# A two-layer attention and mixture-of-experts block on one core: another PSUM bank for one pair of transposes, another issuing engine for eight stores

## Chip, cores and metric

The kernel runs as one program on one core of a Trainium2 chip. The metric is the device time of one execution in microseconds (us); several executions are timed and their median is taken. The names of the engines are those of the profile: PE is TensorE (PEld its weight loads), DVE is VectorE, ACT is ScalarE, POOL is GpSimd, SP is SyncE, which does nothing here but issue DMAs.

## What is computed

512 tokens of width 1024 pass through two layers. Each layer is a token mixer followed by a hierarchical mixture of experts; both are added to the tokens through gates that come from a conditioning vector. The first layer mixes with sliding-window attention and gated linear attention, the second with block attention. The change touches only the norm in front of the experts and the experts themselves:

```
for layer in range(2):
    shift1, scale1, gate1, shift2, scale2, gate2 = split(silu(c) @ ada_w[layer] + ada_b[layer], 6)
    h = rms(x, norm1_w[layer]) * (1 + scale1) + shift1
    x = x + gate1 * mixer[layer](h)
    h = rms(x, norm2_w[layer]) * (1 + scale2) + shift2
    # router: softmax over 4 groups, the best group; in it the best 2 of 8 experts, softmax over the two
    # each expert e of 32, on the tokens that chose it:
    #     y = (silu(h @ w1[e]) * (h @ w3[e])) @ w2[e]          # 1024 -> 512 -> 1024
    x = x + gate2 * sum over the two experts of (gate * y)
```

All values are 32-bit floats. The weights of one expert are 6 MB, those of all experts of one layer 192 MB.

## The kernel before

**Tiling.** The tokens stay in SBUF as `x_t`, four tiles of 128 tokens x 1024. Every expert has a window of 64 slots; two experts make a pair of 128 slots, and a pair's tokens are gathered from a DRAM copy of the normed tokens, `h2d[layer]`, by their numbers.

**The norm in front of the experts** is `norm2` (L574 to L590), called once for each of the four token tiles in each layer. It squares and sums (L576), takes the inverse root (L222 to L228), transposes the tile and copies the transposes out of PSUM (L582), multiplies by the router weights (L586, L587), then writes the normed tile into `t` (L589), a tile of a pool that holds it once under the name `adaacc`, and stores it to `h2d` (L590), 512 KB a time. Since there is one such tile, the L589 of a token tile waits until the store of the tile before it has landed. Before the change the store is issued from ACT's queue. This part, like the attention, is ordered by a scheduler.

**The experts** (L1344 to L1386) are ordered by hand: what is written is what each engine gets. The loop runs over `e` = 0 to 32 (number 32 is a second window of one full expert); `odd = e % 2`, and `pr = e // 2` is the pair. In one pass:

1. `stage1` (L1159): the tokens of the expert by w1 and w3 into the PSUM bank `h13`; then Silu on ACT (L1358).
2. `flip_rows` (L1128): four transposes (L1131) of one half of the *next* pair's tokens into the bank `tr`; four modulations on ACT (L1124) read them out, scaled and shifted, into `xT`.
3. Where `odd`: `gather` for the pair after next (L1107): four small matmuls (L1111) into the bank `num` give the slot numbers, DVE reads them (L1113), and GpSimd issues the indirect DMA (L1115) out of `h2d`.
4. DVE multiplies the Silu by the other half of `h13` (L1365): the gated values `gt`.
5. `combine` 0 and 1 of the expert before: PE (L1197) scatters its outputs into one of four banks `cmb`, and DVE adds them into the tokens (L1200).
6. `flip_hidden` (L1162): two transposes of `gt` (L1166) into a PSUM bank that the caller names, and a copy out of it on DVE (L1168), `gT`. Then `combine` 2 and 3.
7. `stage2` (L1174): `gT` by w2 (L1180) into the bank `py`, scaled on DVE (L1184). Between that and the split into two parts (ACT L1190, POOL or DVE L1191) stand `combine` 4 to 7 and, in every even pass, `flip_sel` (L1143): four transposes (L1147) into the bank `tr`, read by ACT (L1151) and DVE (L1152).

PSUM has eight banks here, all taken: `py`, `h13`, `num` and `tr` once each, `cmb` four times. A bank that is asked for again waits for the readers of what it held.

**The weights** come by 1 MB loads (L178, L181) on SP's queue into a ring of 18 slots, six for each expert, so the stream runs three experts ahead; a slot's next load is issued when its last matmul is done.

Of the kernel before, what the change touches and what calls it, by code (L numbers as in the profile page):

```python
# [74 lines left out]
def tile_hybrid_block(ctx, tc, a, out):  # L75
    nc = tc.nc
    V, S, G, PE, SP = nc.vector, nc.scalar, nc.gpsimd, nc.tensor, nc.sync
# [56 lines left out]
    h2d = [dram.tile([T, D], F32, name=f"h2d{l}") for l in range(2)]  # L134
# [83 lines left out]
    def rsqrt(sm, ss, n, inv, tag, out=None):  # L218
        v = sm.tile([P, n], F32, name=f"rv_{tag}")
        y = sm.tile([P, n], F32, name=f"ry_{tag}")  # L220
        t = sm.tile([P, n], F32, name=f"rt_{tag}")
        V.tensor_scalar(v, ss, inv, 1e-6, op0=OP.mult, op1=OP.add)  # L222
        S.activation(t, v, AF.Ln)
        S.activation(y, t, AF.Exp, scale=-0.5)
        V.scalar_tensor_tensor(t, y, -0.5, y, op0=OP.mult, op1=OP.mult)
        V.tensor_tensor(t, t, v, OP.mult)
        r = y if out is None else out
        V.scalar_tensor_tensor(r, t, 1.5, y, op0=OP.add, op1=OP.mult)  # L228
        return r
# [95 lines left out]
    def transpose_to(ps, blocks, name="pa"):  # L325
        t = ps.tile([P, 512], F32, name=name)
        for i, b in enumerate(blocks):
            PE.transpose(t[:, 128 * i:128 * i + 128], b, ident)
        return t


    for l in range(2):
        s1, s2 = "left", "right"
        tiles = ((0, 1, 2, 3), (3, 2, 1, 0))[l]
        with ExitStack() as att:
# [92 lines left out]
            with ExitStack() as ln:  # L428
# [54 lines left out]
                for k in range(KT):  # L483
# [4 lines left out]
                    t = tmp.tile([P, T], F32, name="ht", bufs=2)  # L488
# [85 lines left out]
            def norm2(tmp, i):  # L574
                ss = sm.tile([P, 1], F32, name="ss2")
                S.activation(tmp.tile([P, D], F32, name="xn2"), x_t[:, i, :], AF.Square, accum_out=ss)  # L576
                rsqrt(sm, ss, 1, 1.0 / D, "l2", out=r2[:, i:i + 1])
                xT = []
                for q in range(2):
                    t = com.tile([P, 4, 128], F32, name=("raw", ("stg", "pt")[l])[q], bufs=2 + l * q)  # L580
                    p = transpose_to(ppA, [x_t[:, i, 512 * q + 128 * k:512 * q + 128 * k + 128] for k in range(4)])
                    (V.tensor_copy, S.copy)[q](t, p.rearrange("p (k t) -> p k t", k=4))  # L582
                    xT.append(t)
                p = ppA.tile([P, 512], F32, name="pa")
                for k in range(KT):
                    PE.matmul(p[:, 0:36], xT[k // 4][:, k % 4, :], wr[:, k, :], start=(k == 0), stop=(k == KT - 1))  # L586
                V.scalar_tensor_tensor(lgt[:, i, :], p[:, 0:36], r2[:, i:i + 1], br, op0=OP.mult, op1=OP.add)  # L587
                t = com.tile([P, D], F32, name="adaacc")
                S.activation(t, x_t[:, i, :], AF.Identity, scale=r2[:, i:i + 1])  # L589
                S.dma_start(h2d[l][128 * i:128 * i + 128, :], t)  # L590

            def flip_strip(dst, kind, h0, hk):

# [6 lines left out]
            if l == 0:  # L600
# [151 lines left out]
                for c in range(7):  # L752
                    i, r0 = c // 2, 64 * (c % 2)
# [92 lines left out]
                out_b(1, oBh, oBl)  # L846
                bg(99)
                norm2(l2t, 0)
                out_b(2, oBh, oBl)
                norm2(l2t, 1)  # L850
# [138 lines left out]
        with ExitStack() as rt:  # L989
# [31 lines left out]
            for g in ((slice(0, 3), slice(3, 4)), (slice(1, 4), slice(0, 1)))[l]:  # L1021
                nt = g.stop - g.start
                if nt == 1:
                    i = g.start
# [79 lines left out]
        def bank(name):  # L1104
            return ps.tile([P, 512], F32, name=name, bufs=4 if name == "cmb" else 1)

        def gather(sel, m):  # L1107

            p = bank("num")
            for i in range(NT):  # L1110
                PE.matmul(p[0:m, 0:2], sel[:, i, :], toknum[:, i, :], start=(i == 0), stop=(i == NT - 1))  # L1111
            num = mu.tile([P, 1], I32, name="num", bufs=2)
            V.tensor_scalar(num[0:m], p[0:m, 0:1], p[0:m, 1:2], 4096.0, op0=OP.add, op1=OP.add)  # L1113
            xg = next(xg_of)
            G.indirect_dma_start(xg[0:m], None, h2d[l][:], bass.IndirectOffsetOnAxis(ap=num[0:m, 0:1], axis=0),  # L1115
                                 bounds_check=T - 1, oob_is_err=False)
            return xg
# [44 lines left out]
        def flip_hidden(gt, psn, eng=S.copy):  # L1162

            p = bank(psn)
            for c2 in range(2):
                PE.transpose(p[:, 128 * c2:128 * c2 + 128], gt[:, 128 * c2:128 * c2 + 128], ident)  # L1166
            gT = mu.tile([P, 2, 128], F32, name="gT")
            eng(gT, p[:, 0:256].rearrange("p (c s) -> p c s", c=2))  # L1168
            return gT
# [36 lines left out]
        def new_xT():  # L1206
            return mt.tile([P, KT, 128], F32, name="xT", bufs=2)
# [112 lines left out]
        def sel_of(pr):  # L1320
            return select((rd if 2 * pr < NK else rd2)[:, :, 2 * pr:2 * pr + 2], 128)

        with tc.manual_schedule():
            sel = sel_of(0)
            xT = new_xT()
            for t in xg_two:
                V.memset(t, 0.0)
            xgs = {0: gather(sel, 128)}
            s2s = {0: flip_sel(sel, 128, "tr")}
            sel = sel_of(1)  # L1330
            xgs[1] = gather(sel, 128)
            pw = bank("py")
            for _ in range(4):
                PE.matmul(pw, ones, cf[:, 0:512], start=True, stop=True)
            for h in range(2):
                flip_rows_fast(xT, h, xgs[0])
            xTs = {0: xT}
            w7 = mk_.tile([P, 7 * E], F32, name="w7")
            n_win = mk_.tile([P, 1], F32, name="n_win")
            V.memset(rd2[:, :, E + 1], -BIG)  # L1340
            search = chain(find_windows(), last_expert())
            pend = None
            NP = E // 2 + 1
            for e in range(E + 1):  # L1344
                pr, odd = e // 2, e % 2

                wt = lambda i, e=min(e, E - 1): ring.get(("w", l, e, i))

                ahead = pr + 2
                if odd and ahead < NP:  # L1350
                    sel = sel_of(ahead)
                p13 = bank("h13")
                for k in range(KT):
                    stage1_k(wt, p13, xTs[pr], 64 * odd, k)
                for i in range(4 * (e != E - 1)):
                    ring.done(("w", l, min(e, E - 1), i))
                gt = mu.tile([P, 256], F32, name="gt")
                S.activation(gt, p13[:, 0:256], AF.Silu)  # L1358
                if pr + 1 < NP:
                    if not odd:  # L1360
                        xTs[pr + 1] = new_xT()
                    flip_rows(xTs[pr + 1], odd, xgs[pr + 1])
                if odd and ahead < NP:
                    xgs[ahead] = gather(sel, 128)
                V.tensor_tensor(gt, gt, p13[:, 256:512], OP.mult)  # L1365
                for j in range(4 * (e > 0)):
                    if j == 2:
                        gT = flip_hidden(gt, "tr", V.tensor_copy)
                    combine(*pend, j)
                if e == 0:  # L1370
                    gT = flip_hidden(gt, "tr", V.tensor_copy)

                def between(e=e, pr=pr, odd=odd, pend=pend):
                    for j in range(4, 8 * (e > 0)):
                        combine(*pend, j)
                    if not odd and pr + 1 < NP:
                        s2s[pr + 1] = flip_sel(sel, 128, "tr")

                y2 = stage2(wt, gT, (V, V) if e == E else (G, V), between=between)
                for i in range(4, 6 * (e != E - 1)):  # L1380
                    ring.done(("w", l, min(e, E - 1), i))
                pend = (lambda i, e=e: (gd if e < NK else gd2)[:, i, e:e + 1], s2s[pr][odd], y2)
                for _ in range(5):
                    next(search, None)
                if e == 2:
                    assert next(search, 0) == 0  # L1386
            nv = nc.values_load(pick[0:1, 1:2], min_val=0, max_val=15)
            spare = [t for t, kind in ring.free if kind == "B"][:6]
            with tc.If(nv > 1):  # L1389
                with tc.For_i(1, nv):  # L1390
                    window()
            if l == 0:
                S.preload_act_table_set("natural_log_exp_and_others")
            for j in range(8):
                combine(*pend, j, tmp={2: "xg", 5: "ytm"}.get(j))
                if l == 1:
                    i, hs = j // 2, slice(512 * (j % 2), 512 * (j % 2) + 512)
                    SP.dma_start(out[0, 128 * i:128 * i + 128, hs], x_t[:, i, hs])
# [111 lines left out]
```

## Time and profile before

| | us |
|---|---|
| median of 3 executions | 1686.16 (1685.32 to 1689.21) |
| the profiled execution's own time | 1688.17 |
| its span in the profile | 1686.3 |

| engine | busy us | share of the span |
|---|---|---|
| PE | 1492.5 | 89% |
| DVE | 1040.5 | 62% |
| PEld | 768.5 | 46% |
| ACT | 512.0 | 30% |
| POOL | 334.3 | 20% |

The profile is of one execution. A group of instructions is named by engine, line and what it writes and reads; the time before it in which its engine stood idle is put down to what ended last before it could begin. The experts of the first layer run from about 331 to 848 us of the span, those of the second from about 1165 to the end. In both stretches the 16 DMA engines are busy nearly all of the time, and PE is busy for more than nine tenths.

### The profile page before, as it was taken

What the parts mean: (1) busy time and instruction counts of PE and PEld (TensorE: products, weight loads), DVE (VectorE), ACT (ScalarE), POOL (GpSimd) and SP (SyncE); (2) the same over time, 40 slices, a digit from 0 to 9 for tenths busy, and PEclk for the clock granted to TensorE, in tenths of its full rate; (3) what the DMA queues carried; (4) which work ended last, traced back from release to release, by engine and by line L of the source; (5) the groups of instructions that cost most, each with busy time, mean ns of one, the idle gap of its engine ahead of it and who ended that gap; (6) DMA issues with size and microseconds to landing.
All of it is one profiled execution on the core that took longest, in us unless ns stands there. A gap on an engine that the chain in (4) does not pass through costs nothing. (4 is left out here: it accounts for less than half of the span.)

```text
span 1686.3 us, 20671 instructions
## 1 busy us (share of the span) xinstructions
PE 1492.5 (89%) x7094; PEld 768.5 (46%) x7094; DVE 1040.5 (62%) x2048; ACT 512.0 (30%) x1163; POOL 334.3 (20%) x260
## 2 busy tenths in 40 slices
PE   5898888789999999999888988997999999999996
PEld 3665566433333333333366765673333333333332
DVE  3678787556556565565568776554755655555555
ACT  4335532322222222222244344532222222222221
POOL 3432252001101111011043432610110110111101
PEclk9989999899999999999989999998999999999999
DMA  8664454799999999998225643239999999999941
GB/s 293 218 238 146 141 199 183 283 412 389 415 419 420 419 421 420 420 420 323 99 66 175 211 138 117 87 147 362 405 387 420 419 418 420 420 420 420 420 188 50
DMA packets 87674, 504.60 MB, mean 299 GB/s; under 512 B 16434, under 2 KB 18656, under 8 KB 33678
## 3 DMA queue, kind: packets, MB, share of 16 engines
q1 hardware_dynamic: 73900, 486.93, 72.5%
q0 software_dynamic: 5088, 8.58, 1.4%
q10 hardware_dynamic: 8578, 7.73, 1.4%
q8 instruction: 58, 0.95, 0.2%
q14 instruction: 50, 0.41, 0.1%
HBM read 506.31 MB, written 6.32 MB: 304 GB/s over the span
## 5 line engine op out<-in xcount | busy, mean ns | idle before, releaser
L1200 DVE SCALAR_TENSOR_TENSOR x<-cmb,gd,x 128x512 f32<-128x512 f32 x524 | 361.7, 742 | 1.4 <-PE cmb L1197 1.4
L1159 PE MATMUL h<-wB,xT 128*64 128x512 f32 x1584 | 353.3, 595 | 0.0
L1191 POOL TENSOR_TENSOR y<-ytm,y 64x512 fp32r<-64x512 f32 x64 | 81.0, 1266 | 775.4 <-ACT y L1190 775.4
L1159 PEld LDWEIGHTS h<-wB,xT 128*64 128x64 f32 x1584 | 109.8, 137 | 212.7 <-issue 204.7
L1197 PE MATMUL cmb<-y,s 128*128 128x512 f32 x528 | 175.8, 436 | 7.9 <-DVEq L1389 7.9
L1180 PE MATMUL py<-wB,gT 128*64 128x512 f32 x736 | 174.5, 617 | 7.1 <-DVE gT L1168 3.9
L349 POOL TENSOR_TENSOR wlo<-wA,whi 128x512 fp32r<-128x512 f32 x86 | 122.4, 1427 | 213.6 <-ACT whi L348 100.9
L1184 DVE TENSOR_TENSOR ytm<-py,g2r 128x512 f32<-128x512 f32 x66 | 45.7, 692 | 173.7 <-issue 144.8
L1190 ACT CAST y<-ytm 64x512 fp32r<-64x512 f32 x132 | 81.4, 617 | 208.6 <-PE cmb L1197 207.0
L368 PE MATMUL pp<-whi,hTh 128*128 128x512 f32 x288 | 118.1, 412 | 5.5 <-ACT raw L405 3.7
L1365 DVE TENSOR_TENSOR gt<-gt,h 128x256 f32<-128x256 f32 x66 | 27.4, 416 | 151.4 <-ACT gt L1358 151.4
L1151 ACT CAST s<-tr 64x512 fp32r<-64x512 f32 x68 | 39.4, 580 | 267.5 <-PE tr L1147 203.9
L1159 PE MATMUL h<-wA,xT 128*64 128x512 f32 x528 | 118.2, 596 | 0.0
L1197 PEld LDWEIGHTS cmb<-y,s 128*128 128x128 f32 x528 | 86.1, 193 | 69.8 <-issue 62.2
L318 DVE SCALAR_TENSOR_TENSOR adaacc<-wC,cond,adaacc 128x1024 f32<-128x1024 f32 x70 | 115.7, 1654 | 1.8 <-DMA wC<-in_ada_w 0.4
L369 PE MATMUL pp<-whi,hTl 128*128 128x512 f32 x288 | 116.2, 406 | 0.5 <-POOL hTl L494 0.4
L1358 ACT ACTIVATE gt<-h 128x256 f32<-128x256 f32 x66 | 25.3, 383 | 293.1 <-PE h L1159 293.1
L1180 PEld LDWEIGHTS py<-wB,gT 128*64 128x64 f32 x736 | 50.3, 141 | 111.1 <-issue 83.7
L1124 ACT ACTIVATE xT<-tr,mc,mc 128x128 f32<-128x128 f32 x256 | 96.2, 456 | 12.4 <-PE tr L1131 12.1
L370 PE MATMUL pp<-wlo,hTh 128*128 128x512 f32 x288 | 92.1, 407 | 0.8 <-POOL wlo L349 0.7
L348 ACT CAST whi<-wA 128x512 fp32r<-128x512 f32 x88 | 54.3, 619 | 88.2 <-PE pp L369 66.9
L1166 PE MATMUL tr<-cf,gt 128*128 128x128 f32 x132 | 29.2, 303 | 58.3 <-ACT xT L1124 39.3
(357 smaller groups left out, 2081.1 us busy)
## 6 DMA issues: line engine op xcount, KB each, us to landing
wB<-in_W SPq DMA_DIRECT2D x278, 1024.0 KB, 11.0
wA<-in_W SPq DMA_DIRECT2D x66, 1024.0 KB, 9.3
wC<-in_ada_w SPq DMA_DIRECT2D x80, 512.0 KB, 5.0
wC<-in_W SPq DMA_DIRECT2D x40, 1024.0 KB, 9.2
wA<-in_WIN SPq DMA_DIRECT2D x21, 1024.0 KB, 4.9
wA<-in_WOUT SPq DMA_DIRECT2D x8, 1024.0 KB, 6.9
wC<-in_ADAC SPq DMA_DIRECT2D x4, 1024.0 KB, 11.7
h2d<-adaacc ACTq DMA_DIRECT2D x8, 512.0 KB, 5.2
```

The source lines that it names most:

```text
L318: V.scalar_tensor_tensor(acc, w, cond[:, k:k + 1], acc, op0=OP.mult, op1=OP.add))
L349: eng.tensor_tensor(lo, src, hi.bitcast(F32), OP.subtract)
L368: PE.matmul(banks[i], hTh[:, k, ts], hi, start=(k == 0), stop=False),
L369: PE.matmul(banks[i], hTl[:, k, ts], hi, start=False, stop=False)),
L370: lambda i, ts: PE.matmul(banks[i], hTh[:, k, ts], lo, start=False, stop=(k == KT - 1)))
L1124: S.activation(dst, src, AF.Identity, scale=sc2[:, kk:kk + 1], bias=sh2[:, kk:kk + 1])
L1159: PE.matmul(p[64 * h:64 * h + 64, :], xT[:, k, off:off + 64], w[:, k % 2, :, 256 * h:256 * h + 256], start=(k == 0), stop=(k == KT - 1), s ...
L1180: PE.matmul(py[64 * h:64 * h + 64, :], gT[:, kt % 2, 64 * (kt // 2):64 * (kt // 2) + 64], w[:, kt % 2, 512 * h:512 * h + 512], start=(kt = ...
L1190: S.copy(y2[h][hs], yt[hs])
L1191: low[h].tensor_tensor(y2[h][ls], yt[hs], y2[h][hs].bitcast(F32), OP.subtract)
L1197: PE.matmul(p, s2[:, 128 * i:128 * i + 128], y2[h], start=True, stop=True)
L1200: V.scalar_tensor_tensor(xs, p, gate(i), xs, op0=OP.mult, op1=OP.add)
```

## The change

It has two parts. The call of `flip_hidden` in the loop over the experts names the bank `num` in place of `tr`, in both places; the call in `window()` (for further windows of full experts, which this input doesn't run) stays. And `norm2` issues its store from GpSimd in place of ACT.

```
             def norm2(tmp, i):
...
                 t = com.tile([P, D], F32, name="adaacc")
                 S.activation(t, x_t[:, i, :], AF.Identity, scale=r2[:, i:i + 1])
-                S.dma_start(h2d[l][128 * i:128 * i + 128, :], t)
+                G.dma_start(h2d[l][128 * i:128 * i + 128, :], t)
...
                 for j in range(4 * (e > 0)):
                     if j == 2:
-                        gT = flip_hidden(gt, "tr", V.tensor_copy)
+                        gT = flip_hidden(gt, "num", V.tensor_copy)
                     combine(*pend, j)
                 if e == 0:
-                    gT = flip_hidden(gt, "tr", V.tensor_copy)
+                    gT = flip_hidden(gt, "num", V.tensor_copy)
```

On PE the order in the loop stays. Here is the end of `stage1` and what follows it in an even pass, before and then after (a row is a line, an operation, what it writes and reads, its shape and how often it stands there):

```order
L1159 MATMUL h_3084<-wB_12_2678,xT 64x512 x4
L1131 MATMUL tr<-cf,xg_2807 128x128 x4
L1197 MATMUL cmb<-y_3058,s_2834 128x512
L1197 MATMUL cmb<-y_3059,s_2834 128x512
L1166 MATMUL tr<-cf,gt 128x128 x2
```

```order
L1159 MATMUL h_3084<-wB_12_2678,xT 64x512 x4
L1131 MATMUL tr<-cf,xg_2807 128x128 x4
L1197 MATMUL cmb<-y_3058,s_2834 128x512
L1197 MATMUL cmb<-y_3059,s_2834 128x512
L1166 MATMUL num<-cf,gt 128x128 x2
```

Before, L1166 waited for DVE (which wrote `gt`) and for ACT (whose modulations L1124 read the bank that L1131 had filled just ahead); now it waits for DVE alone. On DVE the copy `gT` keeps its place behind two of the additions L1200; a piece of the difference there:

```order
 L1365 TENSOR_TENSOR gt<-gt,h_2975 128x256
 L1200 SCALAR_TENSOR_TENSOR x<-cmb,gd,x 128x512 x2
-L1168 COPY gT<-tr 128x256
+L1168 COPY gT<-num 128x256
 L1200 SCALAR_TENSOR_TENSOR x<-cmb,gd,x 128x512 x2
 L1184 TENSOR_TENSOR ytm<-py,g2r 128x512
```

Only the bank that it reads is another. The stores go to POOL, where in the first layer they stand between the last work of the attention and the two first gathers:

```order
 L349 TENSOR_TENSOR wlo<-wA_143,whi 128x512
 L521 TENSOR_TENSOR x<-x,sq 128x512 x4
+L590 DMA h2d_94<-adaacc 128x1024 x4
 L1115 DMA xg_2807<-h2d_94,num 128x1024
 L1115 DMA xg_2808<-h2d_94,num 128x1024
```

On ACT they leave the queue at the end of the first layer's norm, where the scheduler now also puts one copy L582, that of the last token tile, behind an L589:

```order
 L582 COPY stg<-pa 128x512
 L576 ACTIVATE xn_2616,ss_2615<-x 128x1024
-L582 COPY stg<-pa 128x512
 L589 ACTIVATE adaacc<-x,r_91 128x1024
 L223 ACTIVATE rt_l_2620<-rv_l_2618 128x1
-L590 DMA h2d_94<-adaacc 128x1024
+L582 COPY stg<-pa 128x512
 L224 ACTIVATE ry_l_2619<-rt_l_2620 128x1
```

So the copy that the router of the last tile needs now stands behind an instruction that waits for a store's landing.

## Rows read from the trace of the kernel before

**Rows 1.** The page, busy us of each engine, share of the span, instructions.

```profile
PE 1492.5 (89%) x7094; PEld 768.5 (46%) x7094; DVE 1040.5 (62%) x2048; ACT 512.0 (30%) x1163; POOL 334.3 (20%) x260
```

**Rows 2.** Waits: engine, line, awaited: us in total, times, longest us.

```profile
PE tr L1166 <- ACT xT L1124: 39.3, 34, 1.6
...
DVE gT L1168 <- PE tr L1166: 15.8, 34, 1.7
```

**Rows 3.** Timeline, an even pass: start, us, engine, line, form, [idle before <-releaser].

```profile
589.45 0.42 DVE L1365 TENSOR_TENSOR gt<-gt,h 128x256 f32<-128x256 f32 x1 [4.47 <-ACT gt L1358]
589.61 1.50 ACT L1124 ACTIVATE xT<-tr,mc,mc 128x128 f32<-128x128 f32 x4 [0.20 <-PE tr L1131]
589.84 1.41 DVE L1200 SCALAR_TENSOR_TENSOR x<-cmb,gd,x 128x512 f32<-128x512 f32 x2
...
591.17 0.44 PE L1166 MATMUL tr<-cf,gt 128*128 128x128 f32 x2 [1.13 <-ACT xT L1124]
...
591.64 0.42 DVE L1168 COPY gT<-tr 128x256 f32<-128x256 f32 x1 [0.39 <-PE tr L1166]
...
592.12 1.08 PE L1180 MATMUL py<-wB,gT 128*64 128x512 f32 x4
```

**Rows 4.** Timeline, an odd pass with a gather.

```profile
575.39 1.40 DVE L1200 SCALAR_TENSOR_TENSOR x<-cmb,gd,x 128x512 f32<-128x512 f32 x2
...
576.71 0.41 DVE L1168 COPY gT<-tr 128x256 f32<-128x256 f32 x1
...
577.18 0.65 PE L1180 MATMUL py<-wB,gT 128*64 128x512 f32 x2
```

**Rows 5.** Timeline, the first pass of the first layer.

```profile
339.77 0.42 DVE L1365 TENSOR_TENSOR gt<-gt,h 128x256 f32<-128x256 f32 x1 [6.70 <-ACT gt L1358]
...
341.90 0.42 DVE L1168 COPY gT<-tr 128x256 f32<-128x256 f32 x1 [1.71 <-PE tr L1166]
```

**Rows 6.** Windows: PE, PEld, DVE, ACT, POOL busy, granted TensorE clock, DMA share, GB/s.

```profile
341.96:345.37 3.41, 2.99 (x8) 0.99 (x10) 0.36 (x1) 0.00 (x0) 0.00 (x0) 0.50 1.01 423
700.00:750.00 50.00, 46.84 (x218) 18.34 (x216) 27.41 (x45) 11.00 (x24) 4.81 (x4) 1.00 1.01 420
```

**Rows 7.** Landing of the weight loads L181, from 750 to 800 us.

```profile
DMA to landing us min/median/max: 13.9/15.0/15.8
```

**Rows 8.** Timeline, the first layer's last loads (SP), and stage 1 of expert 31.

```profile
756.36 22.13 SPq L181 DMA_DIRECT2D wB<-in_W  x9
...
809.96 2.37 PE L1159 MATMUL h<-wB,xT 128*64 128x512 f32 x10
```

**Rows 9.** Timeline of ACT, the last three stores of the first layer.

```profile
300.97 0.36 ACTq L590 DMA_DIRECT2D h2d<-adaacc  x1
...
308.26 0.33 ACTq L590 DMA_DIRECT2D h2d<-adaacc  x1
310.93 1.15 ACT L589 ACTIVATE adaacc<-x,r 128x1024 f32<-128x1024 f32 x1 [2.10 <-DVE ml L1035]
312.11 0.33 ACTq L590 DMA_DIRECT2D h2d<-adaacc  x1
```

**Rows 10.** Timeline, the first layer's first slot numbers (DVE) and gather (POOL).

```profile
320.15 0.21 DVE L1113 TENSOR_SCALAR num<-num 128x1 int32<-128x1 f32 x1
...
322.84 1.27 POOL L1115 DMA_INDIRECT xg<-h2d,num  x1 [53.10 <-DMA h2d<-adaacc]
```

**Rows 11.** Landing: the stores L590, then the gathers L1115, whole run.

```profile
DMA to landing us min/median/max: 2.6/5.2/7.7
...
DMA to landing us min/median/max: 4.1/8.3/9.8
```

**Rows 12.** Timeline of the second layer: last store, first slot numbers, first gather.

```profile
1145.24 0.33 ACTq L590 DMA_DIRECT2D h2d<-adaacc  x1
...
1156.05 0.21 DVE L1113 TENSOR_SCALAR num<-num 128x1 int32<-128x1 f32 x1
...
1157.02 1.01 POOL L1115 DMA_INDIRECT xg<-h2d,num  x1 [53.62 <-DVE s L1152]
```

More of the change, by code (lines that the diff above doesn't have):

```diff
@@ L589, in norm2 @@
                 S.activation(t, x_t[:, i, :], AF.Identity, scale=r2[:, i:i + 1])
-                S.dma_start(h2d[l][128 * i:128 * i + 128, :], t)
+                G.dma_start(h2d[l][128 * i:128 * i + 128, :], t)
             def flip_strip(dst, kind, h0, hk):
@@ L1367, in tile_hybrid_block @@
                     if j == 2:
-                        gT = flip_hidden(gt, "tr", V.tensor_copy)
+                        gT = flip_hidden(gt, "num", V.tensor_copy)
                     combine(*pend, j)
                 if e == 0:
-                    gT = flip_hidden(gt, "tr", V.tensor_copy)
+                    gT = flip_hidden(gt, "num", V.tensor_copy)
                 def between(e=e, pr=pr, odd=odd, pend=pend):
```

## Prediction

> **What bounds the kernel now.** I read the busy shares first: PE is busy for 89% of the span, DVE for 62% [rows 1]. In the experts' loops PE is busy 46.84 of 50 us at the full granted clock, with the DMA engines at a share of 1.01 and 420 GB/s [rows 6]. So PE sets the pace there, what it can gain is in its gaps, and the weight stream stands close behind it. The list of waits is next. PE's transposes L1166 wait 34 times and 39.3 us in all for ACT's modulations [rows 2]. This tempts: the change takes exactly this wait away, and the view seems to offer 40 us. A wait is worth only what comes earlier behind it, so I went to the timeline of one pass of each kind and looked for what the next matmuls of stage 2 really wait for. That is the copy gT on DVE; stage 2 starts 0.06 us after it ends, in an even pass (592.06, 592.12) [rows 3] as in an odd one (577.12, 577.18) [rows 4].
>
> **Part one, the bank.** In an even pass gt is ready at 589.45 + 0.42 = 589.87. DVE then does two additions until 589.84 + 1.41 = 591.25, while ACT reads the bank tr until 589.61 + 1.50 = 591.11. Only then do the transposes start, at 591.17, and gT at 591.64; DVE stood idle for 0.39 us before it [rows 3]. With the bank num the transposes can go at about 589.95, behind gt and the two combine matmuls. They are done by about 590.4, since they take 0.44. But gT doesn't follow them: in DVE's order it stands behind the two additions in both kernels. How early it can start behind these is seen in the odd pass, where it waits for nothing: additions from 575.39, gT at 576.71, so 1.32 later [rows 4]. In the even pass that is 589.84 + 1.32 = 591.16. The gain is 591.64 - 591.16 = 0.48 us, not the 1.13 of PE's gap; I take 0.47, with 0.39 (the idle time alone) as the lower bound. What is late next is DVE's two additions, and the rest of PE's gap, about 0.65 us, goes from in front of the transposes to the front of stage 2.
>
> In an odd pass with a gather, gt is later (DVE first reads the slot numbers), ACT is done before the additions are, and gT follows them without a gap [rows 4]: gain 0. The pass of expert 31 has no gather and goes like an even one. Pass 0 has no additions ahead of gT: gt ends at 339.77 + 0.42 = 340.19, and gT could start 0.06 for the signal and 0.47 for the transposes later (591.17 to 591.64 [rows 3]), at 340.72 instead of 341.90 [rows 5]: 1.18. Pass 32 transposes no further tokens, so nothing is gained there.
>
> The list of waits has the same count from another side: DVE's gT waits for the transposes 34 times, 15.8 us in all, 1.7 at most [rows 2]. That is 17 passes in each of two layers: 15 even ones (2 to 30), number 31 and number 0. So **the gain is 2 x (16 x 0.47 + 1.18) = 17.4 us**; with 0.39 in place of 0.47 it is 14.8.
>
> The new bank brings two more waits. The transposes must follow DVE's reading of the slot numbers, which stands ahead of gt on DVE anyway, and the slot matmuls of the next odd pass must follow gT, over 10 us earlier. In the other direction flip_sel and the next flip_rows lose gT as the earlier reader of tr. Both cost nothing.
>
> Pass 0 of the first layer has one thing more. From 341.96 to 345.37 the granted clock was 0.50 of full speed, the lower of its two levels, right behind the gap that shrinks [rows 6]. PE did 2.99 us of matmuls there, so at the full level the stretch would be about 1.5 us shorter. Other idle time lies just ahead of that loop, so I give this half a chance: -0.7, with ends at 0 and -1.5.
>
> **The stream.** The weights must follow a pace that is 17.4 us quicker over two layers, 8.7 in each. They run at 420 GB/s with the engines always busy [rows 6], so I let the stream gain nothing, and the landing of a load grows by up to 8.7 us through a layer. The loads for the last experts land 13.9 to 15.8 us after issue [rows 7]; the last is issued by 756.36 + 22.13 = 778.5 and lands by 794.3, and stage 1 of expert 31 starts at 809.96 [rows 8]. That leaves 15.7 us in cover. Of these 8.7 are used up and 7.0 remain, so the stream takes nothing back.
>
> **Part two, the stores.** ACT loses eight issues of 0.33 to 0.36 us [rows 9], all outside the loop; I count them as nothing. POOL gets them where it has nothing else to do, ahead of the first gathers, which wait for the stores anyway [rows 10]. What matters is how long a store from GpSimd takes to land. The trace has none, so I bound it. From ACT a store took 2.6 to 7.7 us [rows 11]; the one issued at 308.26 had landed when L589, which needs its tile, started at 310.93 [rows 9], and the next, under the weight loads, landed not long before the gather at 322.84 [rows 10]. The nearest rows for GpSimd are its gathers, of up to the same 128 rows of 4 KB: 4.1 us when the engines are free, median 8.3, at most 9.8 among weight loads [rows 11].
>
> In the first layer the stores are a chain through one tile: a store, its landing, L589 (1.15), the next store. With 4.1 us for the two stores that go out between load bursts and 8.3 to 9.8 for the last, the first lands at 305.1, before L589 wants the tile (1.18 before its own store at 308.26, as 310.93 is before 312.11, so at 307.08) [rows 9]. The second lands 1.4 to 1.5 us later than now, and the last between 321.9 and 323.4 against about 322.0 (322.84 less 0.86 us for POOL to start a gather, an estimate from the second layer, where the slot numbers end at 1156.05 + 0.21 and the gather starts at 1157.02, 0.76 later [rows 12], and a little more for a landing). That is -0.1 to +1.4. If L589 uses the early landing to move ahead of the copy L582, the chain is up to 1.5 earlier, and then the slot numbers, ready at 320.15 + 0.21 [rows 10], bound the gain at about -1. With s us for every store, the last lands at 300.97 + 3s + 2 x 1.18 (L589 and its issue), which is 3s - 18.7 later than now: at s = 8.3, +6.2. Two of the stores fall where the loads themselves wait for a store (L178 waits for h2d), and that speaks for the low value. I take **+0.5**, with ends at -1 and +6.2.
>
> In the second layer the last store goes at 1145.24, and the gather at 1157.02 waits for the slot numbers, not for the store [rows 12]. With the longest GpSimd landing, 9.8, it would be there at 1155.0, and 0.86 later is still before 1157.02: cost 0.
>
> The Trainium skill has a rule against this part: "DMA: Bandwidth & Descriptors", section "Issuing engine by pattern", sends simple stores to the hardware queues, and its section "Specifications" gives the first byte as about 1 us from GpSimd against 0.6 from ACT or SP. By that alone, as an estimate, three stores in a chain would cost 1.2 us; the free gather against the free store (4.1 against 2.6 us [rows 11]) shows a larger difference, 1.5 for each.
>
> **The sum.** -17.4 - 0.7 + 0.5 = -17.6 us. From the profiled execution's 1688.17 that leads to 1670.6. That execution was 2.0 above the median of the runs shown, 1686.16, so against the median the forecast is **1668.6 us**.
>
> **The rivals.**
> 1. *The stores cost what contended gathers cost.* The 8.3 us are the median of the gathers [rows 11], but most of these run under a full weight stream. Then +6.2 in place of +0.5: 1674.3. Chance 0.18.
> 2. *The weight stream becomes the bound.* For it: the share is 1.01 already [rows 6], and landings are 15 us [rows 7]. Against it: the 7.0 us of cover that remain. Were the landing to grow by 8.7 for the quicker pace and by the whole cover of 15.7 besides, each layer would give back its 8.7, leaving only the change of the stores and clock: 1686. Chance 0.05. The skill's "DMA: Bandwidth & Descriptors", section "Specifications", gives a limit of about 358 GB/s for one core; by it the stream would already be the bound, but it runs at 420 here. Its ceiling of 435 GB/s for the fabric leaves some room above.
> 3. *Slower: one store tile and slow stores.* Each store from GpSimd would have to take s with 3s - 18.7 in the first layer, plus s - 10.9 in the second (the gather at 1157.02, less 0.86, less 1145.24), above the 18.1 gained: that turns at s = 11.9. At s = 13.5 it is 21.8 + 2.6 = 24.4, which gives 1692.5. No landing of GpSimd in the trace passes 9.8 [rows 11]. Chance 0.04.
> 4. *The whole of PE's wait comes back.* 32 x 1.13 + 2 x 1.6, so about 39 us: 1647. For it stands only the list of waits [rows 2]; the order on DVE is against it. Chance 0.04.
> 5. *The change doesn't do what it says*, since gT is held elsewhere in even passes too (by DVE's additions having to wait for their matmuls, say): 1686.7. The idle time of DVE before gT is put down to the transposes alone, against it. Chance 0.03.
>
> **How the numbers follow.** The forecast has 0.66, and its own range is 1664 (a full 1.5 from the clock, 1 from the stores, and 2 for the scatter of the runs shown) to 1672 (14.8 in place of 17.4, no clock). The first rival lies just above. The range that should hold the time 8 times in 10 takes it in, with a little for its own scatter: **1663 to 1677**. What is left out are rivals 2 to 5 and the tails. A measurement of this kernel can tell about 0.2%, 3.4 us, from no change. Faster by more than that: the forecast, rival 1, rival 4 and a part of rival 2 that gives back only some, 0.90. Same: rivals 2 and 5 for the rest, 0.06. Slower: rival 3, 0.04.
>
> **What would show it.** In the profile after, PE's L1166 in even passes should wait for gt (DVE) or nothing, some 1.1 us before where it stands now. gT should follow the additions without idle time, so that the 15.8 us of waits nearly vanish, and stage 2's wait for gT should grow instead. An even pass should be 0.47 us shorter, an odd one unchanged. The landings of the loads late in each layer should be 6 to 9 us longer, and no stage 1 should wait for a load. In the first layer I look at when L589 and the first gather start: the gather within 1.5 us of where it was, relative to the norm's work, says the stores were cheap. I would be wrong if a stage 1 begins to wait for DMA, if the odd passes lengthen by what the even ones gain, or if the first gather slips by 6 us or more.

## The result

The changed kernel takes 1666.78 us (median of 4, 1664.72 to 1671.87) against 1687.26 us for the kernel before (median of 4, 1685.32 to 1689.21): a ratio of 0.9883 with a 95% interval of 0.9857 to 0.9909, so 20 us or 1.2% faster. The forecast was 1668.6.

The page of the changed kernel: PE's busy time is 6.4 us lower, the span 21.8 us shorter.

```profile
span 1664.5 us, 20698 instructions
...
PE 1486.1 (89%) x7094; PEld 768.3 (46%) x7094; DVE 1037.5 (62%) x2048; ACT 512.4 (31%) x1163; POOL 338.6 (20%) x268
```

One more wait of the kernel before (engine, line, awaited: us in total, times, longest us), beside those of [rows 2], is that of the transposes in odd passes, which the list puts down to DVE's additions. In such a pass on the timeline, ACT's reading of tr ends at 576.09, just ahead of them:

```profile
PE tr L1166 <- DVE x L1200: 17.8, 26, 0.7
...
574.58 1.51 ACT L1124 ACTIVATE xT<-tr,mc,mc 128x128 f32<-128x128 f32 x4 [0.20 <-PE tr L1131]
...
576.14 0.44 PE L1166 MATMUL tr<-cf,gt 128*128 128x128 f32 x2 [0.69 <-DVE x L1200]
```

The waits of the changed kernel answer to these. The transposes' wait for ACT is gone, and so is that of the odd passes. DVE's wait for the transposes has fallen from 15.8 us in 34 waits to 1.1 in 2 (pass 0 of each layer). The wait in front of stage 2 has grown from 3.9 to 48.6 us.

```profile
PE py L1180 <- DVE gT L1168: 48.6, 66, 0.8
...
PEld num L1166 <- DVE gt L1365: 12.9, 36, 0.7
...
DVE gT L1168 <- PE num L1166: 1.1, 2, 0.5
```

An even pass of the changed kernel on the timeline, as in [rows 3]: the transposes L1166 start at 579.15, right behind gt and while ACT is still reading the other bank. gT starts 1.32 us after the additions begin, and PE waits 0.81 us for it ahead of stage 2.

```profile
578.67 0.42 DVE L1365 TENSOR_TENSOR gt<-gt,h 128x256 f32<-128x256 f32 x1 [4.47 <-ACT gt L1358]
578.84 1.50 ACT L1124 ACTIVATE xT<-tr,mc,mc 128x128 f32<-128x128 f32 x4 [0.20 <-PE tr L1131]
579.07 1.41 DVE L1200 SCALAR_TENSOR_TENSOR x<-cmb,gd,x 128x512 f32<-128x512 f32 x2
...
579.15 0.44 PE L1166 MATMUL num<-cf,gt 128*128 128x128 f32 x2
...
579.34 0.71 PE L1197 MATMUL cmb<-y,s 128*128 128x512 f32 x2
580.39 0.41 DVE L1168 COPY gT<-num 128x256 f32<-128x256 f32 x1
...
580.86 1.94 PE L1180 MATMUL py<-wB,gT 128*64 128x512 f32 x8 [0.81 <-DVE gT L1168]
```

An odd pass of the changed kernel, as in [rows 4]: the transposes are earlier here as well, but gT again stands 1.32 us behind the start of the additions, as before.

```profile
564.61 1.40 DVE L1200 SCALAR_TENSOR_TENSOR x<-cmb,gd,x 128x512 f32<-128x512 f32 x2
...
564.84 0.41 PE L1166 MATMUL num<-cf,gt 128*128 128x128 f32 x2 [0.16 <-DVE gt L1365]
...
565.93 0.41 DVE L1168 COPY gT<-num 128x256 f32<-128x256 f32 x1
...
566.40 1.51 PE L1180 MATMUL py<-wB,gT 128*64 128x512 f32 x6 [0.68 <-DVE gT L1168]
```

From one Silu (L1358) to the next, an even pass took 15.37 us before and takes 14.89 now, an odd one 15.02 and 15.02. So in both layers every even pass gained 0.48 us in the steady part and no odd pass with a gather gained anything; the pass of expert 31, which has no gather, gained 0.48 as well (14.94 to 14.46).

### The profile page after: what moved, and what is told of

Its sections match the earlier page's. It is cut to its first block, busy times and chain, and to the rows that moved or that the text cites. A ratio compares the mean times of both kernels' runs of the same rounds, so it can differ in the third digit from the quotient of the medians.

```text
span 1664.5 us, 20698 instructions
## 1 busy us (share of the span) xinstructions
PE 1486.1 (89%) x7094; PEld 768.3 (46%) x7094; DVE 1037.5 (62%) x2048; ACT 512.4 (31%) x1163; POOL 338.6 (20%) x268
## 5 line engine op out<-in xcount | busy, mean ns | idle before, releaser
L1200 DVE SCALAR_TENSOR_TENSOR x<-cmb,gd,x 128x512 f32<-128x512 f32 x524 | 361.8, 743 | 1.8 <-PE cmb L1197 1.8
L1180 PE MATMUL py<-wB,gT 128*64 128x512 f32 x736 | 170.9, 607 | 33.7 <-DVE gT L1168 33.7
L1358 ACT ACTIVATE gt<-h 128x256 f32<-128x256 f32 x66 | 25.4, 385 | 293.0 <-PE h L1159 293.0
L1124 ACT ACTIVATE xT<-tr,mc,mc 128x128 f32<-128x128 f32 x256 | 96.4, 457 | 12.3 <-PE tr L1131 12.1
L1180 PE MATMUL py<-wC,gT 128*64 128x512 f32 x320 | 73.1, 598 | 14.9 <-DVE gT L1168 14.9
```

Source lines behind the costliest of these rows:

```text
L1124: S.activation(dst, src, AF.Identity, scale=sc2[:, kk:kk + 1], bias=sh2[:, kk:kk + 1])
L1180: PE.matmul(py[64 * h:64 * h + 64, :], gT[:, kt % 2, 64 * (kt // 2):64 * (kt // 2) + 64], w[:, kt % 2, 512 * h:512 * h + 512], start=(kt = ...
L1200: V.scalar_tensor_tensor(xs, p, gate(i), xs, op0=OP.mult, op1=OP.add)
```

## The experiments

Where a pass length is given, it is the time from one Silu to the next in the steady part of a layer, read from the timeline.

**The two parts apart.** The first run leaves the stores on ACT, the second leaves the transposes in tr:

```
# e1_bank_only, against the changed kernel
-                G.dma_start(h2d[l][128 * i:128 * i + 128, :], t)
+                S.dma_start(h2d[l][128 * i:128 * i + 128, :], t)
# e2_stores_only, in both places
-                        gT = flip_hidden(gt, "num", V.tensor_copy)
+                        gT = flip_hidden(gt, "tr", V.tensor_copy)
```

> Only the bank is changed; the stores stay on ACT. If the bank does all of it (my theory): even passes 0.47 to 0.48 us shorter than before, odd ones the same, pass 0 1.2 us shorter (2.7 with the half-clock stretch gone), so 17.4 to 19 us off the time before, about 1668; the first gather leaves as late behind the norm as before. If the stores gained part of the 20.5 us measured (rival): about 3 us less than that, about 1671.

> Only the stores go to GpSimd; the transposes stay in the bank tr. My theory: no change that can be measured, -1 to +1 us against before; each store lands 3 to 5 us after issue, passes of the loop as long as before. Rival (the stores gain): -3 us, with the first gather leaving 1 to 3 us earlier relative to the start of the norm. Rival (the stores cost what contended gathers cost): +6 us.

With the bank alone: 1668.19 us, a ratio of 0.9856 (0.9835 to 0.9877) to the kernel before on that chip. Its passes are those of the changed kernel, 14.89 and 15.02. With the stores alone: 1687.26 us, a ratio of 0.9980 (0.9964 to 0.9996), and its passes are those of before, 15.37 and 15.02. So the bank is the change. By its median the run with the bank alone gains 24 us (21 to 28), more than the 17.4 to 19 that were expected, although its steady passes are as forecast; the runs of the kernel before lie between 1685 and 1697 us on that chip, between 1685 and 1689 on the first. What the stores bring is small: 3.4 us (0.7 to 6.1) by the medians, 1.3 by the traces, between the expected 1 at most and the rival's 3. In the traces, from the first token tile's L589 in the first layer to the first gather, the two kernels with stores on ACT took 40.0 us (282.8 to 322.8, and 279.9 to 319.9), the two with stores on GpSimd 38.7 (280.5 to 319.2, and 280.6 to 319.2). That is 1.3 us less. In the second layer, the last L589 to the first gather took within 0.3 us of the same in all four.

GpSimd's timeline in the changed kernel at that place, and DVE's slot numbers, show that the first gather no longer waits for the last store, as it did in [rows 10], but for the slot numbers. This last store landed 6.8 us after its issue at 309.39, so at 316.2. The landing of the stores over the whole run stands behind these lines:

```profile
304.59 0.53 POOL L590 DMA_DIRECT2D h2d<-adaacc  x1 [6.54 <-ACT adaacc L589]
309.39 0.53 POOL L590 DMA_DIRECT2D h2d<-adaacc  x1 [4.27 <-ACT adaacc L589]
...
318.10 0.21 DVE L1113 TENSOR_SCALAR num<-num 128x1 int32<-128x1 f32 x1
...
319.18 1.09 POOL L1115 DMA_INDIRECT xg<-h2d,num  x1 [9.25 <-DVE s L1152]
...
DMA to landing us min/median/max: 2.9/4.2/8.9
```

A store from GpSimd thus lands in 2.9 to 8.9 us (to 9.6 in the run with the stores alone). The 2.6 to 7.7 us from ACT [rows 11] are the landings of only two of its eight stores, the first of each layer; for the others the trace has none. At the same two places the stores from GpSimd took 3.0 and 8.9 us, 0.4 and 1.2 longer. A store costs 0.53 to 0.60 us of POOL's time to issue, against 0.33 to 0.36 on ACT.

**Is it DVE's two additions that now hold gT?** If so, one addition fewer ahead of gT should gain. The first try put gT behind one addition and moved combines 2 and 3 into the middle of stage 2; the second is the same with the transposes in tr:

```
# e3_early_gT, against the changed kernel (e4_early_gT_tr: the same with "tr")
-                for j in range(4 * (e > 0)):
-                    if j == 2:
+                for j in range(2 * (e > 0)):
+                    if j == 1:
...
             for kt in range(4):
+                if kt == 2 and mid is not None:
+                    mid()        # combine(*pend, 2), combine(*pend, 3)
```

> The changed kernel, with gT one place further forward on DVE: behind one addition in place of two (combine 1 follows it, combines 2 and 3 go between the two halves of stage 2). Theory: after the change the two additions ahead of gT on DVE are the bound of every pass, so this gains the time of one, 0.66 us, in all 32 passes with additions of each layer: 42 us, about 1625, if the weight stream keeps up. Rival (the stream is the bound once its cover of 13 to 18 us a layer is used): 26 to 36 us, about 1631 to 1641, with stage 1 waiting for loads late in each layer. Rival (something else than these additions holds gT or stage 2): no gain, 1667.

> As the run with gT further forward, but with the transposes in the bank tr. Theory: now the transposes wait for ACT's modulations in every pass, gT comes as late as in the kernel before (odd passes some 0.1 us earlier), so about the time before, 1684 to 1687; the bank is worth 0.48 us in half of the passes when two additions stand ahead of gT, and over 1 us in every even and 0.6 in every odd pass when one does. Rival (the bank matters no more than in the change itself): about 17 us above the run with gT further forward.

Both came out slower than expected. With num: 1679.78 us, 0.9929 (0.9906 to 0.9952) of before, so *slower* than the changed kernel, with passes of 15.05 and 15.20. With tr: 1743.85 us, 1.0296 (1.0269 to 1.0322). The theory that the additions alone hold each pass fell. The timeline of an even pass of the first of these shows why:

```profile
582.04 0.44 PE L1166 MATMUL num<-cf,gt 128*128 128x128 f32 x2
...
582.24 0.47 PE L1199 MATMUL cmb<-y,s 128*128 128x512 f32 x1
...
582.63 0.42 DVE L1168 COPY gT<-num 128x256 f32<-128x256 f32 x1
...
583.11 1.94 PE L1182 MATMUL py<-wB,gT 128*64 128x512 f32 x8 [0.40 <-DVE gT L1168]
...
584.97 0.74 PE L1199 MATMUL cmb<-y,s 128*128 128x512 f32 x2
...
585.64 1.94 PE L1182 MATMUL py<-wB,gT 128*64 128x512 f32 x8
```

gT does come 0.66 us earlier (0.66 behind the start of the additions, not 1.32). But the two combines that used to run while PE waited for gT now stand between the halves of stage 2 and push the second half back by 0.67 us (584.97 to 585.64). From its first matmul to the combines behind it, stage 2 takes 4.4 us with them (583.11 to 587.51), and 3.6 in an even pass of the changed kernel (790.24 to 793.82). What had been free was paid for. PE still waits 0.40 us for gT, with nothing to fill that gap.

The run with tr pays the same: its passes, 16.19 and 15.75, are 0.7 longer than with the old bank and the combines left ahead of stage 2 (15.49 and 15.06, below). Eight more of its passes, of 17.4 to 17.8 us, have a mean granted clock of 0.90, where the passes of usual length have 1.00, and are 1.6 to 1.7 us longer for it. Together that is about 57 us, as far as the two profiled executions are apart (1748.42 and 1690.91).

**The same with the combines left in the gap.** One line is changed, and PE keeps three combines between the transposes and stage 2; the second run has the old bank again:

```
# e5_one_addition, against the changed kernel (e8_one_addition_tr: the same with "tr")
                 for j in range(4 * (e > 0)):
-                    if j == 2:
+                    if j == 1:
```

> The changed kernel with gT behind one addition in place of two, and all four combines still ahead of stage 2 on PE. In the run before it that moved gT forward, gT came 0.66 us earlier, but the two combines that had filled PE's gap ahead of stage 2 then cost about 0.8 us inside it. Theory: after the change gT and PE's combines together bound the start of stage 2, so with the combines left in the gap, stage 2 starts 0.46 us earlier in even passes (PE done with three combines) and 0.33 in odd ones: 25 us off the changed kernel, about 1641. Rival (two additions ahead of gT aren't what holds stage 2): no change, 1667. Rival (the weight stream is the bound): less than 20 us, with stage 1 waiting for loads late in each layer.

> As the run with one addition ahead of gT, but with the transposes in the bank tr, where they wait for ACT's modulations. Theory (before the change two waits ran side by side, ACT's reading of tr and DVE's two additions; each hides the other): with the old bank the one addition gains nothing in even passes, which stay at 15.37 us, and 0.1 us in odd ones, so about 1684, some 53 us above the run with one addition and the bank num. Rival (the order on DVE alone is what gains): 1631 to 1645.

With num: 1631.02 us, 0.9650 (0.9628 to 0.9672) of before, 36 us below the changed kernel where 25 were expected; passes 14.25 and 14.50, so 0.64 and 0.52 shorter. The miss is in my price for a combine on PE: I had taken half of the 0.71 us of a pair, and a third combine adds only 0.24 (three take 0.95), which is 0.11 of the 0.18 missed in an even pass; for the rest, stage 2 starts 0.07 ahead of the end that the profile gives the combines. PE's gap ahead of stage 2 is closed: the waits for gT there are down from 48.6 us to 1.0, and gT (575.91) and the three combines (576.06) are done at nearly the same time. An even pass of it on the timeline:

```profile
574.84 0.75 DVE L1200 SCALAR_TENSOR_TENSOR x<-cmb,gd,x 128x512 f32<-128x512 f32 x1
...
574.92 0.44 PE L1166 MATMUL num<-cf,gt 128*128 128x128 f32 x2
...
575.11 0.95 PE L1197 MATMUL cmb<-y,s 128*128 128x512 f32 x3
...
575.50 0.41 DVE L1168 COPY gT<-num 128x256 f32<-128x256 f32 x1
...
575.99 1.51 PE L1180 MATMUL py<-wB,gT 128*64 128x512 f32 x6
```

With tr: 1689.49 us, 0.9985 (0.9967 to 1.0003), no better than the kernel before, and passes of 15.49 and 15.06. Expected were 15.37 and some 14.92; stage 2 now starts 0.18 us behind the end of gT (590.06 to 590.24), not 0.06 as in [rows 3], with three combines on PE ahead of it in place of two, and that takes about the 0.12 and 0.14 us. Here ACT's reading of the bank holds the transposes and these hold gT, with DVE idle for 1.05 us in an even pass, where it was idle for 0.39 in [rows 3]:

```profile
587.61 1.51 ACT L1124 ACTIVATE xT<-tr,mc,mc 128x128 f32<-128x128 f32 x4 [0.20 <-PE tr L1131]
...
587.84 0.75 DVE L1200 SCALAR_TENSOR_TENSOR x<-cmb,gd,x 128x512 f32<-128x512 f32 x1
...
589.17 0.44 PE L1166 MATMUL tr<-cf,gt 128*128 128x128 f32 x2 [1.37 <-ACT xT L1124]
...
589.64 0.42 DVE L1168 COPY gT<-tr 128x256 f32<-128x256 f32 x1 [1.05 <-PE tr L1166]
```

The run with the stores alone, the changed kernel, and these two make a square; all four have the stores on GpSimd. With two additions ahead of gT, the bank is worth 0.48 us in even passes and 0 in odd ones. With one, it is worth 1.24 (15.49 to 14.25) and 0.56 (15.06 to 14.50), 58 us of the whole. Against the kernel before, the move of gT is worth nothing that can be measured, the bank about 20 us, both together 57, each with the stores on GpSimd. In the kernel before, ACT's bank and DVE's order ran side by side, and each hid most of the other.

**The gated values ahead of the slot numbers, and the weight stream.** In odd passes DVE reads the slot numbers (L1113) before it makes gt. The order is turned, on top of the changed kernel and on top of the run with one addition:

```
# e7_gt_first, against the changed kernel; e6_one_addition_gt, against e5_one_addition
+                V.tensor_tensor(gt, gt, p13[:, 256:512], OP.mult)
                 if odd and ahead < NP:
                     xgs[ahead] = gather(sel, 128)
-                V.tensor_tensor(gt, gt, p13[:, 256:512], OP.mult)
```

> The changed kernel with only this: in odd passes DVE makes the gated values before it reads the slot numbers. Theory: the additions then start when the first combine matmul is done, 0.26 us earlier, and gT with them: odd passes with a gather 0.26 us shorter, even ones the same, 8 us in all, about 1659. Rival (the odd pass is bound by ACT or PE): no change, 1667.

> As the run with one addition, and in odd passes DVE makes the gated values before it reads the slot numbers. Theory: the odd passes' transposes then start 0.5 us earlier, and stage 2 with them, 0.5 x 15 in each layer, some 16 us below the run with one addition, about 1625. Rival (the weight stream, whose cover of 13 to 18 us a layer would be used up by 20 us a layer): the time stays above 1632, and PE waits for loads in the last experts.

On top of the changed kernel: 1664.69 us, 0.9862 (0.9839 to 0.9885); odd passes 14.90, so 0.12 us shorter where 0.26 were expected, since the additions now follow the reading of the slot numbers. The 3.6 us that this gives are near what can't be told apart. On top of one addition: **1622.45 us, 0.9600 (0.9582 to 0.9619)**, the fastest kernel here; odd passes 14.24, as short as the even ones, 8.6 us below the run before it where 16 were expected, because PE is then full. A window over most of the first layer's loop (PE, PEld, DVE, ACT, POOL busy, granted clock, DMA share, GB/s), first of the changed kernel, then of this one:

```profile
410.00:780.00 370.00, 349.35 (x1635) 138.06 (x1632) 217.63 (x347) 90.60 (x199) 44.80 (x38) 1.00 1.01 419
```

```profile
410.00:780.00 370.00, 367.75 (x1716) 146.86 (x1714) 230.88 (x365) 95.08 (x208) 46.06 (x39) 1.00 1.01 420
```

PE is busy for 367.75 of 370 us, so there is next to nothing left in its gaps. The stream runs at 420 GB/s whatever the passes take, which is 14.98 us for the 6.29 MB of one expert. A pass of 14.24 us runs ahead of it by 0.74 us, some 24 us in a layer, and that is paid out of the cover. The waits of PE's weight loads in this kernel show that the cover is nearly used up:

```profile
PEld h L1159 <- DMA wB<-in_W: 3.4, 12, 0.3
...
PEld py L1180 <- DMA wB<-in_W: 0.9, 3, 0.3
```

Waits of 0.3 us, 15 in all, where the changed kernel has none. No pass grows by them: in both layers passes 4 to 30 all take 14.21 to 14.26 us. So the stream is close to being the next bound but is not yet one.

## Why the prediction was right

**The bank, step by step.** gT was forecast 1.32 us after the start of the additions, as in the odd pass of before; it stands at 1.32 in both kinds of pass. The forecast gain of an even pass was 0.47, measured 0.48; of an odd one 0, measured 0.00. Pass 0 was forecast at 1.18: in the second layer, where no half-clock stretch lies in it, it went from 14.33 to 13.15 us, 1.18. So the 17.4 us stand, against the 39 us of PE's own wait that the list of waits offered. The rest of that wait went to the front of stage 2, as forecast: the 48.6 us of waiting for gT there also take in the 17.8 of the odd passes, where the transposes start earlier as well and gT does not.

**The clock.** In the first layer pass 0 went from 15.80 to 13.15 us, 2.65; the part beyond 1.18 is the stretch at half the clock [rows 6], which is gone. It was given half a chance. Of the eight first passes with the bank tr in the traces (two layers of before and of the three runs with tr) three have such a stretch and take 15.8 to 16.04 us, and five take 14.33 or 14.34; of the twelve with num none has one, all take 13.15 or 13.16. So the term is real but comes and goes with the old bank: worth 1.5 us where it falls. That it lies in the first layer of the kernel before is luck. Pass 1 has such a stretch with either bank in all but one of the twenty layers traced. Pass 3 has one in nine of them: in both layers of the kernel before and in neither of the changed kernel, but with num in 4 of 12 and with tr in 5 of 8, so this difference of 1.5 to 1.6 us a layer can't be put to the bank. They scatter the times by a few us.

**The stores.** This is the term that was mis-sized: +0.5 was forecast, with ends at -1 and +6.2, and -1.3 was measured in the first layer. The step that failed took the price of a store from the gathers: 4.1 us for the second and third, which took 4.9 and 2.9, and 8.3 to 9.8 for the last, which took 6.8 (4.2 in the run with the stores alone). By the forecast's own reckoning the last store from ACT took 9.9 us, from 312.11 to about 322.0, more than the 7.7 of [rows 11], which has two landings only. The scheduler also ordered the norm a little differently, as the forecast's lower end had it: the second tile's L589 comes 15.6 us after the first's, not 17.0. But counted from the first L589 the last store goes out only 0.4 us earlier (28.9 for 29.3) and the slot numbers come 0.3 later (37.6 for 37.3). So the 1.3 us come mostly from the last store's landing sooner after its issue, up to the slot numbers, which now bound the gather, near the -1 of that lower end. Why it landed sooner is not shown. The second layer cost 0, as forecast.

**The sum.** From the two profiled executions: 3.4 us were gained up to the first Silu, of which 2.3 lie ahead of the first L589, where nothing of the change is; 11.7 in the first loop (15 x 0.48 + 0.48 + 2.65 and the scatter of passes 1 and 3); 1.9 lost again between the layers, 1.3 of it ahead of the second norm, where nothing was changed; 9.2 in the second loop; 0.6 lost behind it. The loops' 20.9 us are the forecast 17.4, the pass 0 stretch of 1.5, and 2 us of scatter. The forecast of 17.6 lies inside the measured interval of 15 to 24 us. In part that is luck: the bank is right to 0.01 us a pass, but the two small terms missed by 0.8 and 1.8 us, both the same way, and the scatter of passes 1 and 3 (2 us) and what the change doesn't touch (2.3 gained, 1.3 lost) are of that size too.

**The rivals.** The weight stream took nothing back: its cover shrank by about 6 us in a layer, where 8.7 were allowed for. The windows of the second layer (columns as above) show where its stream ends and stage 1 of expert 31 begins, first before, then after:

```profile
1619.00:1623.00 4.00, 3.18 (x20) 1.80 (x18) 2.56 (x6) 1.89 (x5) 1.01 (x1) 1.00 0.53 209
1623.00:1627.00 4.00, 4.00 (x19) 1.50 (x16) 1.50 (x3) 0.00 (x0) 0.00 (x0) 1.00 0.05 17
...
1642.78 3.65 PE L1159 MATMUL h<-wB,xT 128*64 128x512 f32 x16
```

```profile
1603.00:1607.00 4.00, 4.00 (x20) 1.57 (x18) 1.99 (x4) 1.14 (x2) 0.46 (x1) 1.00 0.56 228
1607.00:1611.00 4.00, 4.00 (x22) 1.31 (x20) 2.02 (x4) 0.10 (x1) 0.82 (x1) 1.00 0.02 8
...
1620.86 7.09 PE L1159 MATMUL h<-wB,xT 128*64 128x512 f32 x32
```

The stream ends 16 us earlier, stage 1 begins 21.9 earlier, so of about 20 us of cover, where the forecast had 15.7, some 14 are left. In the first layer the stream thins out 8 us earlier and stage 1 begins 14.6 earlier (809.96 [rows 8], 795.39), though there the next loads, from 782.47, blur its end. How long each load took to land can't be read from the changed kernel's trace, so the longer landings that were forecast stay unshown; that no stage 1 waited for a load was seen. Slow stores didn't happen; the longest landing was 8.9 us and no gather waited for it. That gT is held elsewhere in even passes is ruled out by its 1.32 us. The whole of PE's wait did not come back by the change. With DVE's order changed as well, 57 us come out of the two together, more than the 39 of the list, since odd passes gain then too.

## What to carry to other kernels

A wait in the list is worth only what the next thing in line doesn't hide: find the instruction that the bound engine really waits for (here gT, on DVE), and read from a case in which the suspected wait does not reach it (here the odd pass) how early it could start. Where two waits run side by side, removing one shows little and removing the other nothing; try both together before a change is written off. When work is moved off a gap in which it was free, count it at its full price where it lands.

## What was not expected of the hardware

A plain 512 KB store issued from GpSimd landed 0.4 us later than one from ACT at one place and 1.2 later at the other, the only two that can be compared (3.0 against 2.6, 8.9 against 7.7 us); it also costs more to issue, 0.53 to 0.60 us of POOL against 0.33 to 0.36 of ACT. The run with the stores alone is no longer for it. Of matmuls of 128x512 on PE in a row, one takes 0.47 us on the timeline, two 0.71 and three 0.95, so a further one costs 0.24 us and not its own length.
